# Merged first loads, an earlier warm-up, joined transposes, an ordered numerator and a split last accumulation in a two-layer decoder trunk

## The chip, the cores and the metric

The kernel runs on one core of one Trainium2 chip. The metric is device time in microseconds (us) for one launch of the whole program: the median of three runs.

## The reference

Two post-norm layers work on 256 tokens of width 1024 (float32). Each layer does a half-step SwiGLU feed-forward block, a token mixer beside a 4-head cross-attention into 256 memory tokens, and a second half-step feed-forward block. After each of the three sub-layers comes a LayerNorm:

```python
def swiglu(x, w_gate, w_up, w_down):
    return (silu(x @ w_gate) * (x @ w_up)) @ w_down        # 1024 -> 2816 -> 1024
for l in range(2):
    x = layer_norm(alpha * x + 0.5 * swiglu(x, ...), ...)
    u = x @ w_in                                            # one combined input projection
    tok = short_conv(u) if l == 0 else mlstm(u)             # 768 columns
    xa = cross_attention(u[..., -256:], mem @ w_kv[l])      # 256 columns
    x = layer_norm(alpha * x + concat(tok, xa) @ w_out, ...)
    x = layer_norm(alpha * x + 0.5 * swiglu(x, ...), ...)
```

In the mLSTM mixer of layer 1 each head's output is a numerator divided by the larger of the absolute denominator and a floor, and is then normalised over its 192 columns and multiplied by a sigmoid gate.

## The kernel before

**Precision.** Every float32 operand is split into a high part (ScalarE copies it to a rounded form, line 100) and a low part (VectorE subtracts the high part, line 101). A product is three matmuls: high by high, high by low, low by high (`mm3`, lines 176 to 178), or, in `mmw` (line 184), one 512-column and one 256-column matmul. So every weight tile that comes from memory passes through ScalarE and VectorE before TensorE may use it. The two casts of a 1 MB piece are each done in two halves of 1024 columns.

**Weights.** The list `pieces` holds all weight pieces in the order of their use, nearly all of 1 MB (128 partitions by 2048 columns). `get` traces the piece asked for and the one behind it: a load into one of three `raw` buffers by the SP queue, then the casts into one of five `wh` and five `wl` buffers. A `raw` buffer is free for the next load when its last low cast is done.

**The start.** VectorE clears a tile, ScalarE runs one Silu on one column of it, and 16 warm-up matmuls follow on TensorE (line 149). Then, for each of eight chunks of 128 input rows, SP issues one load of the tokens (128 KB, line 155) and one of the first feed-forward group's weights (256 KB, line 158), and both are cast. The first two groups (`outer`) run the chunk loop outermost, so that TensorE can start on the first chunk: four banks, and for each one 512- and one 256-column matmul. In even chunks the high part of the weight is used first, in odd chunks the low part. The second group's pieces (the third and the fourth of the list) are loaded in halves of 512 KB at line 133.

**The feed-forward blocks.** There are 11 groups of 256 hidden columns. In the three later blocks the first two groups (`xs_groups`) are computed token-major by `gu_xs`, for each half t of the tokens, and turned by two transposes each (`hx`, line 332, evacuated by ScalarE at 335 and VectorE at 336). The list `late` holds these transposes back by one step. Behind group 2 the remaining ones are done, and `down` multiplies groups 0 and 1 into the four output banks, token half 0 first. The last three groups' down products are done per token half and output half (`tail`), and `ln_half` and `ln_finish` follow.

**The mLSTM's end.** `numer(t, a)` computes two heads for a token half: matmuls (line 682), then a chain of small VectorE steps (lines 684 to 690), a power on GpSimd (line 691), and per head a VectorE multiply (line 694) and a ScalarE scaling (line 696). `tokens` transposes the result (line 718), ScalarE (262) and VectorE (263) evacuate it, and `OutProj.part` multiplies it by the four pieces of the output projection.

**What sets the order.** Each engine executes its instructions in one fixed order. That order is not the source's alone: a planner lays the program out by priority (source order) and modelled times, so a cast that is ready in its model can stand between two steps of an earlier chain. `tc.issue_after(ins)` makes the instructions that a block puts on the engine of `ins` stand behind `ins`, on that engine alone.

Of the kernel before, what the change touches and what calls it, by code (L numbers as in the profile page):

```python
# [8 lines left out]
F32 = mybir.dt.float32  # L9
F32R = mybir.dt.float32r  # L10
AF = mybir.ActivationFunctionType
# [3 lines left out]
P = 128  # L15
# [11 lines left out]
SPLIT = 1024  # L27
WARM = 16


@with_exitstack
def trunk(ctx: ExitStack, tc: tile.TileContext, d, out):
# [77 lines left out]
    def trace_piece(first=False):  # L110
        n = state["next"]
        if n >= len(pieces):
            return
        key, src, width = pieces[n]
        raw = rawp.tile([P, 2048], F32, tag="raw", name=f"raw{n}")
        state["next"] = n + 1
        if key == ("mem",):
            nc.sync.dma_start(raw, src)
            made[key] = new_act("memT")
            for q in range(2):  # L120
                split_act(raw[:, 1024 * q:1024 * q + 1024], made[key], 4 * q, 4)
            return
        h = wp.tile([P, 2048], F32R, tag="wh", name=f"wh{n}")
        l = wp.tile([P, 2048], F32R, tag="wl", name=f"wl{n}")
        made[key] = (h, l)
        if first:
            return raw, src, h, l
        if n >= 6:
            nc.sync.dma_start(raw[:, :width], src)
        for c in range(0, width, SPLIT):  # L130
            s = slice(c, min(c + SPLIT, width))
            if n < 6:
                nc.sync.dma_start(raw[:, s], src[:, s])
            split(raw[:, s], h[:, s], l[:, s])
# [10 lines left out]
    dve.memset(warm.bitcast(F32), 0.0)  # L145
    act.activation(warm[:, :1], warm[:, :1].bitcast(F32), AF.Silu)
    wb = mbank("warm")
    for _ in range(WARM):
        pe.matmul(wb[:, :256], warm[:, :P], warm, start=True, stop=True)
    x_raw = [zp.tile([P, D], F32, tag="z", name=f"xraw{q}") for q in range(2)]  # L150
    x0 = new_act("x0")
    first = [trace_piece(first=True) for _ in range(2)]
    for k in range(KC):
        xr = x_raw[k // 4][:, (k % 4) * T:(k % 4) * T + T]
        nc.sync.dma_start(xr, d["xT"][:, k * T:(k + 1) * T])
        raw, src, h, l = first[k // 4]
        s = slice((k % 4) * 512, (k % 4) * 512 + 512)
        nc.sync.dma_start(raw[:, s], src[:, s])
        split_act(xr, x0, k, 1)
        split(raw[:, s], h[:, s], l[:, s])  # L160
    cur = {"x": x0}
# [51 lines left out]
    def ln_half(i, t, h, y):  # L213
        if h == 0:
            lns[i, t] = (zp.tile([P, D], F32, tag="z", name=f"z{i}_{t}"),
                         sp.tile([P, 2, 6], F32, tag="st", name=f"st{i}_{t}"))
        z, st = lns[i, t]
        s = slice(512 * h, 512 * h + 512)
        dve.scalar_tensor_tensor(z[:, s], xnat[:, t, s], ALPHA, y, op0=ALU.mult, op1=ALU.add)
        dve.bn_stats(st[:, h, :], z[:, s])  # L220

    def ln_finish(i, t, gb, nx):
        z, st = lns.pop((i, t))
        mv = sp.tile([P, 2], F32, tag="mv", name=f"mv{i}_{t}")
        dve.bn_aggr(mv, st)
        r = rstd_of(mv[:, 1:2], 1, f"ln{i}_{t}")
# [9 lines left out]
        def transposes():  # L236
            for h in range(2):
# [4 lines left out]
                to_parts(nx, 4 * h, 4, t, b)  # L242
        return transposes

    def norm_both(i, gb, nx, tail):
# [20 lines left out]
    def ffn(l, j, xs_groups, i, last=False):  # L266
# [82 lines left out]
        for t in range(2):  # L349
            for g in range(xs_groups):  # L350
                late.append(gu_xs(g, t, pending if (t, g) == (0, xs_groups - 1) else None))
                if len(late) > 1:
                    late.pop(0)()
# [16 lines left out]
        def tail(t):  # L370
            for h in range(2):
                for g in range(NG - TAIL, NG):
                    down(g, t, (h,), ws[g])
                ln_half(i, t, h, y[t, h])
        norm_both(i, gb, nx, tail)


# [178 lines left out]
    def mlstm_mixer(mix, i):  # L556
# [113 lines left out]
        def numer(t, a):  # L670
# [18 lines left out]
            dve.scalar_tensor_tensor(v, r, EPS, r, op0=ALU.mult, op1=ALU.mult)  # L689
            dve.tensor_add(v, v, mv[:, :, 1])  # L690
            pool.tensor_tensor(r, v, mhalf[:, :2], op=ALU.pow)
            for c in range(2):
                o = ogs[t][:, DH * (2 * a + c):DH * (2 * a + c) + DH]
                dve.scalar_tensor_tensor(o, bv[:, c, :DH], mv[:, c, 0:1], o,
                                         op0=ALU.subtract, op1=ALU.mult)
                act.activation(o, o, AF.Copy, scale=r[:, c:c + 1])

# [53 lines left out]
        numer(0, 1)  # L751
        numer(1, 1)
        o.part(1, 1, (0, 1))
        for t in range(2):
            o.part(2, t, (0, 1), (0,))
        tokens(0, 1)
# [39 lines left out]
def _layouts(i):  # L796
# [5 lines left out]
    def colmajor(w, width):  # L802
# [3 lines left out]

    a["xT"] = c(i["x"][0].T.reshape(KC, P, T).transpose(1, 0, 2).reshape(P, KC * T))
    a["memT"] = c(i["mem"][0].T.reshape(KC, P, T).transpose(1, 0, 2).reshape(P, KC * T))
# [3 lines left out]
    g = g.reshape(2, 2, 2, 4, P, 2, NG, 256)  # L812
    a["wgu"] = c(g.transpose(0, 1, 6, 2, 4, 3, 5, 7).reshape(2, 2, NG, 2, P, 2048))
    a["wd"] = c(i["ffn_w_down"].reshape(2, 2, NG, 2, P, D).transpose(0, 1, 2, 4, 3, 5)
                .reshape(2, 2, NG, P, 2048))
# [32 lines left out]
```

## Time and profile before

| what | us |
|---|---|
| median of three runs (lowest, highest) | 987.87 (987.80, 988.37) |
| the profiled execution's own time | 988.58 |
| its span, first to last instruction | 986.4 |
| TensorE (PE) busy | 974.4 |
| VectorE (DVE) busy | 663.5 |
| ScalarE (ACT) busy | 528.9 |
| GpSimd (POOL) busy | 20.4 |

The profiled execution took 2.2 us more than its span, which lies around the first and last instruction, and 0.7 us more than the median. Matmuls are pipelined and their ends are modelled: what counts is the distance from one start to the next. "PEld" is the weight load, "SPq" an issue on the SP queue.

### The profile page before, as it was taken

To read this page: it belongs to the slowest core of one execution; us is meant where nothing else is said; L and a number is where in the kernel's file an instruction comes from. 1 tells how busy PE (TensorE), PEld (TensorE's weight loads), DVE (VectorE), ACT (ScalarE), POOL (GpSimd) and SP (SyncE) were. 2 spreads that over 40 slices of the span, in tenths; PEclk is the share of its full clock that TensorE was granted. 3 is DMA by queue.
4 is the path that set the end of the run, shared out by engine and by line. 5 is a ranking of instruction groups with operands and counts; after the bars stand their busy time and mean duration, and the time that the engine had idled before them with its cause. 6 is when DMAs were issued, how large, how long until landed. Compare 5 with 4: busy or idle time off the path is not lost.

```text
span 986.4 us, 13151 instructions
## 1 busy us (share of the span) xinstructions
PE 974.4 (99%) x5212; PEld 831.8 (84%) x5212; DVE 663.5 (67%) x1014; ACT 528.9 (54%) x847; POOL 20.4 (2%) x30
## 2 busy tenths in 40 slices
PE   8999999999999999999999999999999999999996
PEld 7888888888888888888888888889989778888885
DVE  6685657868667756565865656567878787566565
ACT  6665555447535545555455646445776446454540
POOL 0000000000000000000000000001000000000000
PEclk9999999999999999999999999999999999999999
DMA  8884646466444654646474555534425646546421
GB/s 284 315 302 167 217 168 218 170 225 219 165 155 173 248 202 149 228 153 214 145 282 171 183 201 176 198 113 149 162 95 198 247 175 242 202 154 221 164 86 44
DMA packets 29294, 186.92 MB, mean 189 GB/s; under 512 B 3632, under 2 KB 4656, under 8 KB 8368
## 3 DMA queue, kind: packets, MB, share of 16 engines
q1 hardware_dynamic: 28944, 185.55, 52.8%
q8 instruction: 41, 0.67, 0.3%
q10 hardware_dynamic: 288, 0.52, 0.1%
q14 instruction: 21, 0.17, 0.1%
HBM read 185.01 MB, written 1.05 MB: 189 GB/s over the span
## 4 chain that ended last, share of the span: by engine, by line
PE 97%; DMA 1%; DVE 1%; SPq 0%; ACT 0%; issue 0%; POOL 0%; DVEq 0%; POOLq 0%
PE gu L184 42%; PE y L176 8%; PE y L178 8%; PE y L177 8%; PE gx L176 2%; PE gx L178 2%; PE gx L177 2%; PE cx L184 2%; PE cg L184 2%; PE cb L184 2%; PE yo L178 1%; PE yo L177 1%; PE yo L176 1%; PE qkp L411 1%; PE qkp L412 1%; PE qkp L413 1%
## 5 line engine op out<-in xcount | busy, mean ns | idle before, releaser
L101 DVE TENSOR_TENSOR wl<-raw,wh 128x1024 fp32r<-128x1024 f32 (+1 forms) x342 | 400.1, 1196 | 147.0 <-ACT wh L100 146.4
L100 ACT ACTIVATE wh<-raw 128x1024 fp32r<-128x1024 f32 (+1 forms) x342 | 337.4, 1033 | 100.5 <-PE y L178 47.3
L184 PE MATMUL gu<-x,wh 128*128 128x512 f32 x1216 | 389.1, 395 | 0.0
L184 PEld LDWEIGHTS gu<-x,wl 128*128 128x128 f32 x1216 | 228.4, 188 | 52.9 <-DVE wl L101 1.8
L184 PE MATMUL gu<-x,wl 128*128 128x256 f32 x1216 | 243.3, 278 | 0.8 <-DVE wl L101 0.8
L184 PEld LDWEIGHTS gu<-x,wh 128*128 128x128 f32 x1216 | 189.6, 189 | 3.3
L176 PE MATMUL y<-wh,h 128*128 128x512 f32 x352 | 137.9, 392 | 0.0
L177 PE MATMUL y<-wl,h 128*128 128x512 f32 x352 | 137.0, 389 | 0.0
L178 PE MATMUL y<-wh,h 128*128 128x512 f32 x352 | 136.8, 390 | 0.0
L189 DVE TENSOR_TENSOR s<-s,gu 128x256 f32<-128x256 f32 x152 | 63.0, 417 | 101.7 <-ACT s L188 101.5
L188 ACT ACTIVATE s<-gu 128x256 f32<-128x256 f32 x152 | 57.5, 379 | 103.2 <-PE gu L184 103.2
L178 PEld LDWEIGHTS y<-wh,h 128*128 128x128 f32 x352 | 66.0, 188 | 14.3 <-DVE h L304 0.4
L177 PEld LDWEIGHTS y<-wl,h 128*128 128x128 f32 x352 | 66.1, 188 | 13.7
L176 PEld LDWEIGHTS y<-wh,h 128*128 128x128 f32 x352 | 66.1, 188 | 13.0 <-ACT h L303 0.7
L303 ACT ACTIVATE h<-s 128x256 fp32r<-128x256 f32 x76 | 31.7, 418 | 65.2 <-DVE s L300 64.9
L299 ACT ACTIVATE s<-s 128x256 f32<-128x256 f32 x76 | 31.7, 417 | 38.3 <-DVE s L189 38.3
L304 DVE TENSOR_TENSOR h<-s,h 128x256 fp32r<-128x256 f32 x76 | 32.0, 421 | 17.1 <-ACT h L303 16.9
L262 ACT ACTIVATE x<-xt 128x512 fp32r<-128x512 f32 x20 | 11.4, 596 | 51.4 <-PE xt L241 51.0
L176 PE MATMUL gx<-wh,x 128*128 128x512 f32 x96 | 38.3, 398 | 0.0
L177 PE MATMUL gx<-wl,x 128*128 128x512 f32 x96 | 37.5, 391 | 0.0
L178 PE MATMUL gx<-wh,x 128*128 128x512 f32 x96 | 37.5, 392 | 0.0
L300 DVE SCALAR_TENSOR_TENSOR s<-s 128x256 f32<-128x256 f32 x76 | 32.0, 421 | 1.4
(185 smaller groups left out, 977.5 us busy)
## 6 DMA issues: line engine op xcount, KB each, us to landing
raw<-in_wgu SPq DMA_DIRECT2D x83, 1024.0 KB, 4.8
raw<-in_wd SPq DMA_DIRECT2D x43, 1024.0 KB, 4.8
raw<-in_wconv SPq DMA_DIRECT2D x10, 1024.0 KB, 4.8
raw<-in_wout SPq DMA_DIRECT2D x8, 1024.0 KB, 4.8
raw<-in_wm SPq DMA_DIRECT2D x7, 1024.0 KB, 4.8
gb<-in_lngb SPq DMA_DIRECT2D x6, 1024.0 KB, 4.8
raw<-in_wkv SPq DMA_DIRECT2D x4, 1024.0 KB, 4.8
raw<-in_wop SPq DMA_DIRECT2D x4, 776.0 KB, 4.2
```

Source lines behind the costliest of these rows:

```text
L100: act.activation(h, raw, AF.Copy)
L101: dve.tensor_sub(l, raw, h.bitcast(F32))
L176: pe.matmul(o, ah, bh, start=start, stop=False)
L177: pe.matmul(o, ah, bl, start=False, stop=False)
L178: pe.matmul(o, al, bh, start=False, stop=stop)
L184: pe.matmul(o, w[part], b, start=(k, part) == (0, 0), stop=(k, part) == (KC - 1, 0))
L188: act.activation(o, bank[:, T:], AF.Copy)
L189: dve.tensor_add(o, o, bank[:, :T])
L299: act.activation(t_[:, :256], t_[:, :256], AF.Silu)
L300: dve.scalar_tensor_tensor(t_[:, 256:], t_[:, :256], 0.5, t_[:, 256:], op0=ALU.mult, op1=ALU.mult)
L303: act.activation(hh, t_[:, 256:], AF.Copy)
L304: dve.tensor_sub(hT[g][:, 1, fc, :], t_[:, 256:], hh.bitcast(F32))
```

## The change

The tokens and the first weights are laid side by side in one array (`xw`), so that one load per chunk brings both (384 KB). The first two chunks land in the two `z` buffers, the other six in the three `raw` buffers, two in each. The warm-up no longer waits for ScalarE, and has 20 matmuls; the Silu that loads ScalarE's table runs on a tile of its own, cleared by GpSimd. The transposes held in `late` are done two at a time. In `numer` the multiply and the scaling stand behind the chain of small steps, and the output projection's parts behind the last `numer` have their VectorE casts put behind that chain. In the last block, the last token half's second output half is accumulated in two steps for its last two groups: first columns 0 to 255, in the old bank, then columns 256 to 511, in a bank of their own, and `ln_close` adds the second in.

```diff
-WARM = 16
+WARM = 20
...
-    act.activation(warm[:, :1], warm[:, :1].bitcast(F32), AF.Silu)
     wb = mbank("warm")
     for _ in range(WARM):
         pe.matmul(wb[:, :256], warm[:, :P], warm, start=True, stop=True)
-    x_raw = [zp.tile([P, D], F32, tag="z", name=f"xraw{q}") for q in range(2)]
     x0 = new_act("x0")
     first = [trace_piece(first=True) for _ in range(2)]
+    CH = T + 512
+    xw = [zp.tile([P, D], F32, tag="z", name=f"xw{q}") for q in range(2)]
+    xw += [rawp.tile([P, 2048], F32, tag="raw", name=f"xw{q}") for q in range(2, 5)]
+    table = sp.tile([P, 1], F32, tag="table", name="table", bufs=1)
+    pool.memset(table, 0.0)
+    act.activation(table, table, AF.Silu)
     for k in range(KC):
-        xr = x_raw[k // 4][:, (k % 4) * T:(k % 4) * T + T]
-        nc.sync.dma_start(xr, d["xT"][:, k * T:(k + 1) * T])
-        raw, src, h, l = first[k // 4]
+        q, o = (k, 0) if k < 2 else (1 + k // 2, k % 2 * CH)
+        nc.sync.dma_start(xw[q][:, o:o + CH], d["xw"][:, k * CH:(k + 1) * CH])
+        h, l = first[k // 4]
         s = slice((k % 4) * 512, (k % 4) * 512 + 512)
-        nc.sync.dma_start(raw[:, s], src[:, s])
-        split_act(xr, x0, k, 1)
-        split(raw[:, s], h[:, s], l[:, s])
+        split_act(xw[q][:, o:o + T], x0, k, 1)
+        split(xw[q][:, o + T:o + CH], h[:, s], l[:, s])
...
+    def ln_close(i, t, y, y2):
+        z, st = lns[i, t]
+        dve.scalar_tensor_tensor(z[:, 512:], xnat[:, t, 512:], ALPHA, y, op0=ALU.mult, op1=ALU.add)
+        dve.bn_stats(st[:, 1, :], z[:, 512:768])
+        dve.tensor_add(z[:, 768:], z[:, 768:], y2)
+        dve.bn_stats(st[:, 2, :], z[:, 768:])
...
-                if len(late) > 1:
+                if len(late) > 2:
+                    late.pop(0)()
                     late.pop(0)()
...
+            down(NG - TAIL, t, (1,), ws[NG - TAIL])
+            y2 = mbank("ylast")[:, :256]
+            ends = [(g, fc) for g in range(NG - TAIL + 1, NG) for fc in range(2)]
+            for q, o in enumerate((y[1, 1][:, :256], y2)):
+                for n, (g, fc) in enumerate(ends):
+                    s = slice(fc * D + 512 + 256 * q, fc * D + 768 + 256 * q)
+                    mm3(o, (hT[g][:, 0, fc, tsl(t)], hT[g][:, 1, fc, tsl(t)]),
+                        (ws[g][0][:, s], ws[g][1][:, s]), (q, n) == (1, 0), n == len(ends) - 1)
+            ln_close(i, t, y[1, 1], y2)
...
-            dve.tensor_add(v, v, mv[:, :, 1])
+            chain = dve.tensor_add(v, v, mv[:, :, 1])
             pool.tensor_tensor(r, v, mhalf[:, :2], op=ALU.pow)
-            for c in range(2):
...
+            with tc.issue_after(chain.ins):
+                for c in range(2):
...
+            return chain.ins
...
-        numer(1, 1)
-        o.part(1, 1, (0, 1))
-        for t in range(2):
-            o.part(2, t, (0, 1), (0,))
+        with tc.issue_after(numer(1, 1)):
+            o.part(1, 1, (0, 1))
+            for t in range(2):
+                o.part(2, t, (0, 1), (0,))
```

## Rows read from the trace of the kernel before

**Rows 1.** The page: busy time, share and instructions of each engine, and the shares of the chain that ended last.

```profile
PE 974.4 (99%) x5212; PEld 831.8 (84%) x5212; DVE 663.5 (67%) x1014; ACT 528.9 (54%) x847; POOL 20.4 (2%) x30
...
PE 97%; DMA 1%; DVE 1%; SPq 0%; ACT 0%; issue 0%; POOL 0%; DVEq 0%; POOLq 0%
```

**Rows 2.** The chain that ended last, in order of time, two pieces of its start: start, duration, what.

```profile
9.33 7.19 DMA raw<-in_wgu
...
18.92 11.05 PE gu L184 x62
```

**Rows 3.** The timeline of TensorE at the start: start, duration, engine, line, operation, out<-in, shape, count (rows of one kind are merged), and in brackets the idle time and what ended it.

```profile
2.27 3.74 PE L149 MATMUL warm<-warm 128*128 128x256 f32 x16 [2.27 <-ACT warm L146]
5.85 0.41 PE L184 MATMUL gu<-x,wh 128*128 128x512 f32 x1
...
7.15 0.28 PE L184 MATMUL gu<-x,wl 128*128 128x256 f32 x1
8.19 0.38 PE L184 MATMUL gu<-x,wl 128*128 128x256 f32 x1 [0.76 <-DVE wl L101]
...
17.98 0.86 PE L184 MATMUL gu<-x,wh 128*128 128x512 f32 x3
18.92 0.51 PE L184 MATMUL gu<-x,wl 128*128 128x256 f32 x2
```

**Rows 4.** The timeline of ScalarE and VectorE in the same stretch: the clearing of the warm-up tile, and the casts of the first chunks.

```profile
0.85 0.27 DVE L145 MEMSET warm<- 128x256 f32 x1 [0.85 <-PEq L840]
...
4.40 0.63 ACT L100 ACTIVATE wh<-raw 128x512 fp32r<-128x512 f32 x1 [0.76 <-DMA raw<-in_wgu]
...
5.07 0.69 DVE L101 TENSOR_TENSOR wl<-raw,wh 128x512 fp32r<-128x512 f32 x1 [0.97 <-ACT wh L100]
...
5.55 0.42 ACT L100 ACTIVATE x<-xraw 128x256 fp32r<-128x256 f32 x1 [0.52 <-DMA xraw<-in_xT]
...
6.78 0.63 ACT L100 ACTIVATE wh<-raw 128x512 fp32r<-128x512 f32 x1 [0.81 <-DMA raw<-in_wgu]
...
7.44 0.69 DVE L101 TENSOR_TENSOR wl<-raw,wh 128x512 fp32r<-128x512 f32 x1 [1.02 <-ACT wh L100]
```

**Rows 5.** The timeline of the SP queue: the issues of the first chunk's tokens and of the second chunk's weights (those of the first chunk's weights and of the second's tokens lie between).

```profile
0.73 0.39 SPq L155 DMA_DIRECT2D xraw<-in_xT  x1
...
2.10 0.43 SPq L158 DMA_DIRECT2D raw<-in_wgu  x1
```

**Rows 6.** Two stretches of the table by windows: stretch and length, busy time and instructions of each engine, granted clock, share of the DMA engines, GB/s. The rows loaded in the first are 1 and 2 KB long, in the second 4 KB.

```profile
2.00:4.00 2.00, 1.73 (x8) 1.73 (x9) 0.33 (x1) 0.62 (x3) 0.00 (x0) 1.00 0.89 230
...
16.00:18.00 2.00, 2.00 (x14) 1.65 (x13) 1.02 (x2) 1.45 (x3) 0.00 (x0) 1.00 1.06 404
```

**Rows 7.** The timeline of TensorE behind the last numerators.

```profile
782.46 0.39 PE L178 MATMUL yo<-wh,mix 128*128 128x512 f32 x1
782.69 0.49 PE L718 MATMUL tk<-ident,og 128*128 128x128 f32 x3
783.76 0.50 PE L176 MATMUL yo<-wh,mix 128*128 128x512 f32 x1 [0.58 <-ACT mix L262]
...
785.64 0.39 PE L178 MATMUL yo<-wh,mix 128*128 128x512 f32 x1
```

**Rows 8.** The timelines of VectorE, GpSimd and ScalarE there: the last step of the last numerator's chain and the cast ahead of it, two of the four powers, and the scaling that the transposes wait for.

```profile
781.26 1.23 DVE L101 TENSOR_TENSOR wl<-raw,wh 128x1024 fp32r<-128x1024 f32 x1 [0.65 <-ACT wh L100]
782.40 0.15 DVE L690 TENSOR_TENSOR dv<-dv,hmv 128x2 f32<-128x2 f32 x1
...
778.48 0.69 POOL L691 TENSOR_TENSOR dn<-dv,mhalf 128x2 f32<-128x2 f32 x1 [18.20 <-DVE dv L690]
782.73 1.51 POOL L691 TENSOR_TENSOR dn<-dv,mhalf 128x2 f32<-128x2 f32 x1 [3.56 <-DVE dv L690]
...
784.28 0.80 ACT L696 ACTIVATE og<-og,dn 128x192 f32<-128x192 f32 x2 [0.57 <-POOL dn L691]
```

**Rows 9.** The timeline of TensorE around one pair of transposes (the matmul before, and the second matmul behind), and one piece of the chain with eight transposes.

```profile
503.42 0.39 PE L178 MATMUL gx<-wh,x 128*128 128x512 f32 x1
...
504.10 0.39 PE L177 MATMUL gx<-wl,x 128*128 128x512 f32 x1
...
310.53 0.87 PE xt L241 x8
```

**Rows 10.** The second feed-forward block, behind group 2: VectorE's low part of the last transposes, and the fifteenth matmul of `down` on TensorE.

```profile
337.95 0.42 DVE L336 TENSOR_TENSOR h<-hx,h 128x256 fp32r<-128x256 f32 x1
...
338.82 0.39 PE L178 MATMUL y<-wh,h 128*128 128x512 f32 x1
```

**Rows 11.** The end of the kernel: two VectorE steps of the timeline, two groups of VectorE instructions by shape (busy time, mean ns of one, idle time before), and two pieces of the chain, a matmul of 256 columns and one of 512, each up to the next one's start.

```profile
978.65 0.69 DVE L219 SCALAR_TENSOR_TENSOR z<-xnat,y 128x512 f32<-128x512 f32 x1 [2.34 <-PE y L178]
979.37 0.69 DVE L220 BATCH_NORM_STATS2 st<-z 128x6 f32<-128x512 f32 x1
...
L189 DVE TENSOR_TENSOR s<-s,gu 128x256 f32<-128x256 f32 x152 | 63.0, 417 | 101.7 <-ACT s L188 101.5
L684 DVE BATCH_NORM_STATS2 hst<-num 128x6 f32<-128x192 f32 x8 | 2.6, 353 | 1.1 <-PE num L682 1.1
...
759.96 0.12 PE qkp L413
...
970.00 0.23 PE y L177
```

More of the change, by code (lines that the diff above doesn't have):

```diff
@@ L114, in trace_piece @@
         key, src, width = pieces[n]
-        raw = rawp.tile([P, 2048], F32, tag="raw", name=f"raw{n}")
         state["next"] = n + 1
+        if not first:
+            raw = rawp.tile([P, 2048], F32, tag="raw", name=f"raw{n}")
         if key == ("mem",):
@@ L126, in trace_piece @@
         if first:
-            return raw, src, h, l
+            return h, l
         if n >= 6:
@@ L215, in ln_half @@
             lns[i, t] = (zp.tile([P, D], F32, tag="z", name=f"z{i}_{t}"),
-                         sp.tile([P, 2, 6], F32, tag="st", name=f"st{i}_{t}"))
+                         sp.tile([P, 3, 6], F32, tag="st", name=f"st{i}_{t}"))
         z, st = lns[i, t]
@@ L224, in ln_finish @@
         mv = sp.tile([P, 2], F32, tag="mv", name=f"mv{i}_{t}")
-        dve.bn_aggr(mv, st)
+        dve.bn_aggr(mv, st if nx is None and t == 1 else st[:, :2, :])
         r = rstd_of(mv[:, 1:2], 1, f"ln{i}_{t}")
@@ L371, in tail @@
             for h in range(2):
+                if last and (t, h) == (1, 1):
+                    break
                 for g in range(NG - TAIL, NG):
@@ L374, in tail @@
                 ln_half(i, t, h, y[t, h])
+            else:
+                return
+            down(NG - TAIL, t, (1,), ws[NG - TAIL])
[7 more added lines that the diff above has]
+            ln_close(i, t, y[1, 1], y2)
         norm_both(i, gb, nx, tail)
@@ L689, in numer @@
             dve.scalar_tensor_tensor(v, r, EPS, r, op0=ALU.mult, op1=ALU.mult)
-            dve.tensor_add(v, v, mv[:, :, 1])
+            chain = dve.tensor_add(v, v, mv[:, :, 1])
             pool.tensor_tensor(r, v, mhalf[:, :2], op=ALU.pow)
-            for c in range(2):
[L693 to L696, printed above, removed]
+            with tc.issue_after(chain.ins):
+                for c in range(2):
+                    o = ogs[t][:, DH * (2 * a + c):DH * (2 * a + c) + DH]
+                    dve.scalar_tensor_tensor(o, bv[:, c, :DH], mv[:, c, 0:1], o,
+                                             op0=ALU.subtract, op1=ALU.mult)
+                    act.activation(o, o, AF.Copy, scale=r[:, c:c + 1])
+            return chain.ins
         v1 = [hp.tile([P, NH, DH + 1], F32, tag="h", name=f"v1_{t}") for t in range(2)]
@@ L805, in colmajor @@
         return c(w.reshape(KC, P, n, width).transpose(2, 1, 0, 3).reshape(n, P, KC * width))
-    a["xT"] = c(i["x"][0].T.reshape(KC, P, T).transpose(1, 0, 2).reshape(P, KC * T))
     a["memT"] = c(i["mem"][0].T.reshape(KC, P, T).transpose(1, 0, 2).reshape(P, KC * T))
@@ L813, in _layouts @@
     a["wgu"] = c(g.transpose(0, 1, 6, 2, 4, 3, 5, 7).reshape(2, 2, NG, 2, P, 2048))
+    xT = i["x"][0].T.reshape(KC, P, T).transpose(1, 0, 2)
+    w0 = a["wgu"][0, 0, 0].reshape(2, P, 4, 512).transpose(1, 0, 2, 3).reshape(P, KC, 512)
+    a["xw"] = c(np.concatenate([xT, w0], axis=2).reshape(P, KC * (T + 512)))
     a["wd"] = c(i["ffn_w_down"].reshape(2, 2, NG, 2, P, D).transpose(0, 1, 2, 4, 3, 5)
```

## The prediction

> **What bounds the kernel now.** I read the page first: TensorE is busy for 974.4 of 986.4 us, and the chain that ended last runs for 97% through it [rows 1]. So nothing that spares ScalarE, VectorE or a transfer in the middle is worth anything by itself; time can come only from the 12 us in which TensorE doesn't work, and from TensorE instructions that go. Then I read the chain in order of time, and TensorE's timeline where it isn't on that chain. There are three such places. At the start the chain passes through the load of the third weight piece (7.19 us from its issue) before TensorE takes it over at 18.92 for good [rows 2]. Behind the last numerators TensorE waits twice within 3 us [rows 7]. At the end VectorE works alone, normalising the last half [rows 11]. All terms are made against the profiled execution, 988.58 us (a span of 986.4 and 2.2 around it), which lies 0.71 above the median of 987.87; I carry the sum over to the median. No change of this kernel below 0.2% (1.98 us) is told from none here.
>
> **The start.** Now: 16 warm-up matmuls begin at 2.27, behind ScalarE, and the first real one at 5.85 [rows 3]: (5.85 - 2.27) / 16 = 0.22 each for 256 columns, where 256 columns later take 0.12 [rows 11]. [...] The last matmul of chunk 0 starts at 7.15 and takes 0.12, and the next starts at 8.19: 0.92 lost, since chunk 1 begins with the low part of its weights, whose cast runs from 7.44 to 8.13 [rows 3, 4]. Just before 18.92, three matmuls of 0.23 from 17.98 end at 18.67: 0.25 lost to the third piece's casts; between the two places I count 0.1 more in uneven spacings, an estimate. [...] ScalarE's Silu on its own tile costs nothing: ScalarE has no other work until the first load lands. The first load's issue stays at 0.73, and the second chunk's weights, issued at 2.10 now [rows 5], go with the second load, one issue of about 0.45 behind the first: near 1.2. The chunk's weights now land at about 4.38 and 6.76, which is where ScalarE stops waiting for them [rows 4]. A load of 384 KB lands as a whole, so the tokens' cast (0.42) no longer runs ahead of the weights: that is the change's own cost. A chunk's low part is ready at its landing plus 0.42 + 0.63 + 0.69 and three hand-overs, 1.9 together. The rows loaded grow from 1 and 2 KB to 3 KB; the 1 and 2 KB rows went at 230 GB/s with the DMA engines 0.89 busy, 4 KB rows at 404 [rows 6]; I take 330 for 3 KB, nearer the middle than either end. Then the first chunk lands near 4.1 and the second, 393 KB and 1.2 us behind it plus what several loads in flight cost each other, near 5.7. Chunk 0 starts near 5.3, and chunk 1's low part is ready at 7.6 in place of 8.13. From there TensorE has 1.4 us of work per chunk against about 1.2 of load and 1.1 of casts on either engine, so it doesn't wait again. Gain: 0.55 at chunk 1, the 0.35 behind it, and 0.1 because the third piece no longer shares the queue with the last chunks: 1.0. Ends: 0, if the second chunk lands as now; at most the 1.27 lost plus 0.5 of earlier start, 1.8. A loss is possible too, since the third piece's buffer is free only when chunk 3 is cast: it would be requested near 10 instead of 9.33 [rows 2], 0.7 later, all of which could reach TensorE.
>
> [...]
>
> **Joined transposes.** A pair costs TensorE this: from 503.42 to 504.10 there are 0.68 us and two matmuls of 0.23, which leaves 0.22, or 0.11 for one transpose; eight in a row take 0.87, again 0.11 each [rows 9]. So a visit has no cost of its own that joining could save: 0. Ends: a gain of 0.02 for each of two visits saved in three blocks, 0.1; a loss if the evacuation comes late. Group 0's transposes for token half 1 now come behind group 2 with those of group 1. They are needed from the thirteenth matmul of `down` on, their low part in the fifteenth, which starts at 338.82; VectorE finishes the low part there at 338.37 [rows 10]. The cover is 0.45 us in the order of now.
>
> **Numerators.** From 782.69 to 785.64 TensorE does six transposes (6 x 0.11) and five matmuls (5 x 0.23): 1.8 of 2.95 us, so 1.15 are lost [rows 7]. The first wait, 0.58, is for ScalarE's evacuation of the first transposes. The second is for the last numerator's scaling at 784.28, behind a power of 1.51, behind a chain step at 782.40 that stood behind a cast of 1.23 [rows 8]. With the chain ahead of the multiplies and of the output projection's casts I expect that step near 780, two to three us earlier; the power takes 0.70 and the scaling 0.80 [rows 8], so the second token half is ready by 783, when TensorE has done the first three transposes. All six then follow one another, the evacuation's wait stays, and the sixth matmul starts at 783.76 + 5 x 0.23 = 784.9 instead of 785.64. I take 0.65. Ends: a gain of 1.15 if the planner moves the transposes ahead of other work; a loss, because the edge holds back the casts of the output projection's last piece (two of 1.23) until the chain is done, with everything behind them in VectorE's queue. If the step stays at 782.40, they end near 784.9, and the first triple's third matmul, which needs VectorE's evacuation behind them, comes about 1.2 late. The casts of the next block aren't in that block and may still cut in.
>
> **The end.** Twelve matmuls of 512 columns become 24 of 256: 24 x 0.12 - 12 x 0.23 = +0.12. Behind the last one VectorE now adds 512 columns (0.69) and takes their statistics (0.69) [rows 11]. After, that work on the finished columns lies beside the second 12 matmuls (1.44), and an add of 256 columns (0.42) and statistics of 256 remain; 192 columns take 0.35, so 0.40 [rows 11]. 1.41 - 0.03 - 0.82 is a gain of 0.56, less 0.12 and about 0.04 for a wider aggregate: 0.4. Ends 0.2 and 0.6: only VectorE's first two steps running over the 1.44 could shorten it, and they take 1.1.
>
> **The sum.** -1.0 - 0 - 0.65 - 0.4 = -2.05: 986.5 for the profiled execution, and 985.8 against the median.
>
> **The rivals.** *The start is held by its transfers:* the DMA engines are 0.9 busy from 2 us on [rows 6], one load must bring tokens and weights before anything is cast, and the third piece is asked for later. The gain there is 0, the rest 1.05: 986.8. Against it stands that 404 GB/s is reached with longer rows. *The numerators gain nothing:* the held casts or the next block's stand beside the power. The power took 0.69 once and 1.51 when a cast of two SBUF operands ran beside it [rows 8]; forcing casts directly behind the chain invites just that, and the 0.65 is used up. The sum is -1.4: 986.5. [...] *More than that, at the start and the numerators:* the second chunk lands at 5.4 (0.3 more), and the planner, with an earlier chain in its model, lifts the transposes so that the 0.58 goes too: -2.95, 984.9. *Slower:* the joined transposes' low part comes too late. At three blocks VectorE would have to finish two evacuations where one had 0.45 us to spare; one more pair of casts (2 x 1.23) ahead of them costs 2.46 + 0.42 - 0.45 = 2.4 each, one cast 1.2. With one cast in each block, +3.6 - 2.05 = +1.55: 989.4, with two in one of them 990.6. It decides from 0.45 us of delay on. Against it: the evacuation stands ahead of the next cast in all likelihood, since it comes earlier in the source.
>
> **How the numbers follow.** The forecast has 0.48, and its own range of 985.0 to 986.7 lies across the bound at 985.89, two thirds below it: 0.32 faster, 0.16 same. The better case has 0.15, faster. The held start (0.15) and the idle numerators (0.14) are within 0.2%. The slower case has 0.08, 0.05 of it above 989.85. That gives 0.47 faster, 0.48 same, 0.05 slower. The range leaves out most of the slower case and the outer ends of the start: 984.3 to 988.0.
>
> **What would show it.** The start: TensorE's first real matmul near 5.3, chunk 1 near 7.6, and the work that is at 18.92 now near 17.9. The transposes: four in 0.44 and no wait in `down`. The numerators: the chain's last step near 780, and no wait for the scaling. The end: from the last matmul's start to the aggregate 1.3 in place of 1.9. It is wrong if chunk 1 starts at 8.1 or later, if new waits for VectorE appear on TensorE behind group 2, or if the planner's order has changed far from the edits.

## The result, and the profile after

The changed kernel is slower: 990.47 us (median of 11 executions, 989.55 to 993.69) against 988.20 for the kernel before (11 executions, 987.73 to 989.06), a ratio of 1.0025 with a 95% interval of 1.0017 to 1.0033. That is 2.3 us the wrong way, 4.7 above the forecast of 985.8 and 2.5 above the upper end of its range, 988.0. The profiled execution of the changed kernel took 992.05 (span 989.8). TensorE's granted clock fell once in it, and its mean over the span is 0.994, as in the slowest execution (993.69); the nine others have 0.997 or 0.998. How far the fall counts is told with the experiments.

Read in the order of time, three of the four places went about as forecast. The start, from TensorE's timeline and from the chain that ended last (start, duration, what; idle time and its releaser in brackets):

```profile
5.47 0.63 PE L189 MATMUL gu<-x,wh 128*128 128x512 f32 x2
...
7.33 0.40 PE L189 MATMUL gu<-x,wh 128*128 128x512 f32 x1
...
9.88 0.80 PE L189 MATMUL gu<-x,wl 128*128 128x256 f32 x2
```

```profile
2.10 6.45 DMA xw<-in_xw
...
10.29 18.54 PE gu L189 x104
...
34.30 10.81 PE gu L189 x62
```

The first real matmul is at 5.47 (5.85 before) and chunk 1 has begun by 7.33 (8.19) [rows 3]. A fourth load now lands at 8.55 and holds TensorE a last time near 9.9. From 10.29 it runs without a stop, past the place near 18.9 where the chain of before was still waiting [rows 2]. The group that starts at 34.30 started at 35.43 before: 1.13 gained. But that is one profile against one. e2 and e8 (below) keep the start of before, and their profiles reach the same group earlier than that of the kernel before; here are before, e2 and e8, from the same chain:

```profile
35.43 11.18 PE gu L184 x64
```

```profile
34.53 11.18 PE gu L184 x64
```

```profile
34.80 11.18 PE gu L184 x64
```

The ten profiles with the new start lie between 33.93 and 34.77. So the profile that the forecast was made from was the latest of three, and by these thirteen profiles the usual gain is nearer to half a microsecond.

The joined transposes, one group of them in the chain of the second feed-forward block:

```profile
334.21 0.44 PE hx L345 x4
```

Four transposes take 0.44, 0.11 each as in [rows 9], and no matmul behind them waits.

The numerators, from the timelines of TensorE, VectorE and GpSimd:

```profile
782.01 0.82 PE L747 MATMUL tk<-ident,og 128*128 128x128 f32 x6
783.08 0.50 PE L181 MATMUL yo<-wh,mix 128*128 128x512 f32 x1 [0.25 <-ACT mix L275]
```

```profile
777.23 0.69 POOL L718 TENSOR_TENSOR dn<-dv,mhalf 128x2 f32<-128x2 f32 x1 [16.69 <-DVE dv L717]
779.16 0.69 POOL L718 TENSOR_TENSOR dn<-dv,mhalf 128x2 f32<-128x2 f32 x1 [1.24 <-DVE dv L717]
```

The chain's last step came at 778.83 instead of 782.40 [rows 8], both powers took 0.69, all six transposes follow one another, and 0.25 of marked waiting is left where the kernel before has 0.58 [rows 7] and 0.29:

```profile
784.78 0.33 PE L718 MATMUL tk<-ident,og 128*128 128x128 f32 x1 [0.29 <-ACT og L696]
...
792.70 0.39 PE L178 MATMUL yo<-wh,mix 128*128 128x512 f32 x1
793.02 1.29 PE L241 MATMUL xt<-ident,xnat 128*128 128x128 f32 x8
```

The lead over the kernel before grows from 0.68 at the transposes (782.69 - 782.01) to 1.52 at the last `yo` matmul (792.70 - 791.18): 0.84 gained.

Then all of it is lost, and more, within 10 us. TensorE behind that point:

```profile
791.18 0.39 PE L183 MATMUL yo<-wh,mix 128*128 128x512 f32 x1
794.49 1.94 PE L246 MATMUL xt<-ident,xnat 128*128 128x128 f32 x8 [2.92 <-DVE xnat L236]
797.29 0.63 PE L181 MATMUL gx<-wh,x 128*128 128x512 f32 x1
...
800.89 0.39 PE L181 MATMUL gx<-wh,x 128*128 128x512 f32 x1
```

The transposes of the normalised tokens (`xt`) wait 2.92 us for VectorE's `xnat`; the kernel before has no such wait, as its row at 793.02 above shows. The table by windows (length, busy time of PE, PEld, DVE, ACT, POOL, granted clock, DMA share, GB/s) shows what came behind the wait:

```profile
794.00:796.00 2.00, 1.51 (x7) 1.54 (x8) 2.00 (x4) 0.38 (x1) 0.00 (x0) 0.50 0.00 0
...
800.00:802.00 2.00, 2.00 (x9) 1.63 (x8) 2.00 (x4) 0.00 (x0) 0.28 (x1) 0.85 0.78 262
```

The two stretches between them show 0.50 as well. From 797.29 to 800.27 the `gx` matmuls start 0.43 apart, from 800.89 on, with a granted clock of 1.00 from 802 to 804, 0.23. The second set of eight transposes starts at 807.9; before it was 804.1.

VectorE in the same stretch, with the ten microseconds ahead of it:

```profile
770.34 0.56 DVE L693 SCALAR_TENSOR_TENSOR decays<-ms,decays 128x384 f32<-128x384 f32 x1 [4.94 <-PE ms L692]
772.02 0.56 DVE L693 SCALAR_TENSOR_TENSOR decays<-ms,decays 128x384 f32<-128x384 f32 x1 [1.12 <-PE ms L692]
775.41 0.63 DVE L711 BATCH_NORM_STATS2 hst<-num 128x6 f32<-128x192 f32 x2 [2.83 <-PE num L709]
...
779.56 3.49 DVE L101 TENSOR_TENSOR wl<-raw,wh 128x1024 fp32r<-128x1024 f32 x3
...
784.00 2.35 DVE L101 TENSOR_TENSOR wl<-raw,wh 128x1024 fp32r<-128x1024 f32 x2
...
786.86 1.22 DVE L101 TENSOR_TENSOR wl<-raw,wh 128x1024 fp32r<-128x1024 f32 x1
...
789.57 0.69 DVE L224 SCALAR_TENSOR_TENSOR z<-xnat,yo 128x512 f32<-128x512 f32 x1 [0.30 <-PE yo L183]
...
791.61 0.69 DVE L224 SCALAR_TENSOR_TENSOR z<-xnat,yo 128x512 f32<-128x512 f32 x1
792.22 0.15 DVE L211 TENSOR_SCALAR ln_0v<-mv 128x1 f32<-128x1 f32 x1
...
793.60 1.41 DVE L236 SCALAR_TENSOR_TENSOR xnat<-z,ln_0r,gb 128x512 f32<-128x512 f32 x2
```

VectorE stands idle for 8.9 us (4.94 + 1.12 + 2.83) ahead of the numerators, and then runs six casts of weights between 779.56 and 788.0, the last one between two steps of token half 0's LayerNorm. At 791.61 a step of token half 1 stands ahead of half 0's `ln_0v`, which needed nothing by then but its place in the queue. That step reads what the last `yo` matmul has written, so it could not start before TensorE had run out of work. In the chain it stands, and no cast, between that matmul and half 0's path:

```profile
791.35 0.24 PE yo L183
...
791.61 0.69 DVE z L224
```

From 791.61 to `xt` at 794.49 there are 2.9 us, the whole wait of this profile. So half 1's step sets the end of the wait here; the cast at 786.86 and the step of half 1 at 789.57, which itself waits for TensorE, delay half 0's statistics ahead of it. The held casts hold their buffers too, and so the loads behind them. ScalarE, which makes the high part first, waits for data there:

```profile
791.77 2.00 ACT L100 ACTIVATE wh<-raw 128x1024 fp32r<-128x1024 f32 x2 [3.03 <-DMA raw<-in_wgu]
```

The end, VectorE behind the last matmul, which starts at 982.28:

```profile
982.60 0.42 DVE L255 TENSOR_TENSOR z<-z,ylast 128x256 f32<-128x256 f32 x1 [0.29 <-PE ylast L183]
...
983.52 0.24 DVE L230 BATCH_NORM_AGGREGATE mv<-st 128x2 f32<-128x18 f32 x1
```

From the last matmul's start to the aggregate there are 1.24 us, in place of 1.88 (980.10 - 978.22) before, whose steps of 512 columns are in [rows 11]. From the first of the last half's matmuls to the end of the span it is 15.71 instead of 16.11: 0.40 gained.

So the trace gives -1.13, 0, -0.84 and -0.40 where -1.0, 0, -0.65 and -0.4 were forecast, and a wait of 2.92 with a fall of the clock behind it that was not in the sum. The places add up: 1.52 ahead of the kernel before at the last `yo` matmul, 1.47 behind at `xt`, 3.8 behind at the second set, and 3.4 behind at the end of the span. (Of the start's 1.13 only 0.68 were left at the numerators. Most of the rest goes near 680, where the chain of this profile passes through a load of weights, 5.30 us from 670.95, and that of before does not.) My theory: the edges shift VectorE's queue, so that casts stand ahead of half 0's LayerNorm, on which TensorE then waits. The rivals: the loss is a ripple of the start or the transposes; the numerators' own order makes it; or half 1's steps make it and the casts don't matter.

### The profile page after: what moved, and what is told of

Read it like the earlier page. It is cut to its first block, busy times and chain, and to the rows that moved or that the text cites. A ratio compares the mean times of both kernels' runs of the same rounds, so it can differ in the third digit from the quotient of the medians.

```text
span 989.8 us, 13168 instructions
## 1 busy us (share of the span) xinstructions
PE 977.7 (99%) x5228; PEld 836.0 (84%) x5228; DVE 664.2 (67%) x1016; ACT 528.5 (53%) x847; POOL 19.6 (2%) x31
## 4 chain that ended last, share of the span: by engine, by line
PE 96%; DMA 2%; DVE 1%; ACT 0%; issue 0%; SPq 0%; DVEq 0%; ACTq 0%
PE gu L189 42%; PE y L181 8%; PE y L183 8%; PE y L182 8%; PE gx L181 2%; PE gx L182 2%; PE gx L183 2%; PE cx L189 2%; PE cg L189 2%; PE cb L189 2%; PE yo L181 1%; PE qkp L438 1%; PE yo L182 1%; PE yo L183 1%; PE qkp L439 1%; PE qkp L440 1%
## 5 line engine op out<-in xcount | busy, mean ns | idle before, releaser
L101 DVE TENSOR_TENSOR wl<-raw,wh 128x1024 fp32r<-128x1024 f32 x334 | 394.4, 1207 | 141.8 <-ACT wh L100 141.1
L100 ACT ACTIVATE wh<-raw 128x1024 fp32r<-128x1024 f32 x334 | 332.3, 1042 | 95.0 <-PE y L183 28.5
L181 PE MATMUL y<-wh,h 128*128 128x512 f32 (+1 forms) x352 | 137.5, 391 | 0.0
L182 PE MATMUL y<-wl,h 128*128 128x512 f32 (+1 forms) x352 | 136.6, 388 | 0.0
L183 PE MATMUL y<-wh,h 128*128 128x512 f32 (+1 forms) x352 | 136.5, 389 | 0.0
```

Source lines behind the costliest of these rows:

```text
L100: act.activation(h, raw, AF.Copy)
L101: dve.tensor_sub(l, raw, h.bitcast(F32))
L181: pe.matmul(o, ah, bh, start=start, stop=False)
L182: pe.matmul(o, ah, bl, start=False, stop=False)
L183: pe.matmul(o, al, bh, start=False, stop=stop)
```

## The experiments

All ratios are against the kernel before on the same chip. In e1, e3, e4, e5, e6, e9, e10 and e11 the changed kernel is the base, in e2, e7 and e8 the kernel before.

**e1: without both edges.**

```diff
-            with tc.issue_after(chain.ins):
-                for c in range(2):
+            for c in range(2):
...
-        with tc.issue_after(numer(1, 1)):
-            o.part(1, 1, (0, 1))
+        numer(1, 1)
+        o.part(1, 1, (0, 1))
```

> The changed kernel without its two edges on VectorE (the multiplies of og may stand between the chain's steps again, and the casts of the output projection's last piece are no longer kept behind the chain); start, joined transposes and end stay. Theory (the held casts push the casts of the next weights into the LayerNorm of token half 0): TensorE's idle time of 2.92 us before the transposes xt near 794 goes, the granted clock behind it stays near 1.00, and the time is that of the kernel before less what start and end give, 988.2 - 1.1 - 0.4 = 986.7, 986.0 to 987.4. Rival 1 (the loss is a ripple of the start or of the joined transposes, and the edges only happen to stand there): the idle time and the low clock stay, near 990.5. Rival 2 (start and end give nothing in timed runs): 988.2.

Measured: 987.03 (986.87 to 987.39), ratio 0.9985, interval 0.9976 to 0.9993. The casts are back in VectorE's free time (the first pair and the last of five are shown, two single ones lie between), and `xt` follows the last `yo` matmul (791.42) without a wait:

```profile
764.73 2.35 DVE L101 TENSOR_TENSOR wl<-raw,wh 128x1024 fp32r<-128x1024 f32 x2
...
773.15 1.23 DVE L101 TENSOR_TENSOR wl<-raw,wh 128x1024 fp32r<-128x1024 f32 x1 [1.16 <-ACT wh L100]
```

```profile
791.75 1.29 PE L246 MATMUL xt<-ident,xnat 128*128 128x128 f32 x8
```

The five casts (2.35 + 3 x 1.22, 6.0 us of work) stand where the changed kernel has 8.9 us of nothing. Both rivals of this run fall: the loss sits in the edges, and the other three parts together are a gain.

**e2: the kernel before, with nothing but the casts held.**

```diff
-        numer(1, 1)
+        with tc.issue_after(numer(1, 1)):
+            o.ws[2] = get("wo", 1, 2)
         o.part(1, 1, (0, 1))
```

> The kernel before with one thing added: the low casts of the output projection's last piece stand behind the chain of numerator (1,1) on VectorE; the numerators are as before, and so are start, transposes and end. Theory (held casts alone make the loss): an idle time of 1.5 to 3 us before xt, a granted clock near 0.5 behind it, and 1.5 to 4 us more than before: 989.7 to 992.2. Rival (the order inside the numerators makes it): 988.2, no idle time before xt over 0.3 us.

Measured: 990.52 (989.82 to 991.73), ratio 1.0020, interval 1.0011 to 1.0029. The numerators' own steps keep their order of before, and the wait is there; behind it, in the profiled execution, the `gx` matmuls start 0.43 apart from 795.86 to 798.84, as they do in the changed kernel at a granted clock of 0.50:

```profile
782.88 0.50 PE L176 MATMUL yo<-wh,mix 128*128 128x512 f32 x1 [0.25 <-ACT mix L262]
...
793.88 1.29 PE L241 MATMUL xt<-ident,xnat 128*128 128x128 f32 x8 [2.51 <-DVE xnat L231]
```

So holding the casts is enough to make the loss. It is enough for the numerators' gain too: no cast stands between the chain's steps any more, the six transposes follow one another, and the wait behind them is the 0.25 of the changed kernel.

**e10 and e11: one edge each.** These two complete the square. e10 takes away the outer edge only, e11 the inner one only.

> The changed kernel without the outer edge alone (the casts of the output projection's last piece are free), the inner one (multiplies of og behind the chain) stays. VectorE's order then has four casts of weights between the chain's steps of the last two numerators, and one cast and one z and bn_stats of half 1 among the steps of half 0's LayerNorm. Theory (each cast in a chain costs its 1.2 us where the chain is waited for): the transposes tk of token half 1 wait again as in the kernel before, xt waits 0.5 to 2 us, and the time lies between e1 and the changed kernel, 987.3 to 989.5. Rival (the inner edge gives its gain without the outer one): 986.0 to 986.8.

> The changed kernel without the inner edge alone (the multiplies of og may stand between the chain's steps), the outer one stays: with e1 (neither edge), e10 (inner only) and the changed kernel (both) this fills the square. VectorE's order has two held casts, one more, and two z of half 1 (one of them between the steps of half 0) and a cast ahead of half 0's normalisation, as in e2. Theory: the wait before xt is that of e2 (2.5 us, clock falling in a part of the executions), and the time is e2's 990.5 less what start and end give, 1.3: 989.2, 988.5 to 990.2. Rival (only the inner edge does harm): 987.0.

Measured: e10 992.40 (990.59 to 993.30, 5 executions), ratio 1.0037, interval 1.0024 to 1.0051; e11 990.61 (988.87 to 991.08), ratio 1.0019, interval 1.0010 to 1.0028. Both lie above what the theory expected, e10 by 2.9 us and e11 by 0.4, and both rivals fall. `xt` waits 2.51 us in e11, as in e2. In e10 the output projection's casts ran early, but VectorE's order has other casts inside the last numerators' chains and one ahead of half 0's normalisation, where it waited for its high part:

```profile
792.84 1.23 DVE L101 TENSOR_TENSOR wl<-raw,wh 128x1024 fp32r<-128x1024 f32 x1 [0.36 <-ACT wh L100]
793.99 1.41 DVE L234 SCALAR_TENSOR_TENSOR z<-z,mv,gb 128x512 f32<-128x512 f32 x2
```

```profile
796.20 1.29 PE L246 MATMUL xt<-ident,xnat 128*128 128x128 f32 x8 [3.13 <-DVE xnat L236]
```

The held casts are therefore a sufficient cause and not the only one: either edge alone changes the planner's order of VectorE's queue, and each of these orders puts something ahead of half 0's path. What the theory has to say is "whatever stands in the queue ahead of half 0", not "the held casts". The square also parts the gain: the numerators' waits are 0.25 with the outer edge alone (e11), and 0.58 and 0.53 with the inner edge alone (e10), no less than before. The gain comes with the casts being held back, and so does the wait that ate it.

**e6: half 1's LayerNorm steps kept behind half 0's.** The edit names only the order of these steps.

```diff
+        with tc.issue_after(done[0]) if i == 4 and t == 1 else ExitStack():
+            dve.scalar_tensor_tensor(z[:, s], xnat[:, t, s], ALPHA, y, op0=ALU.mult, op1=ALU.add)
+            dve.bn_stats(st[:, h, :], z[:, s])
...
+            done[0] = dve.scalar_tensor_tensor(xnat[:, t, s], z[:, s], r, gb[:, 1, s],
+                                               op0=ALU.mult, op1=ALU.add).ins
```

> The changed kernel with the same edge alone (half 1's z and bn_stats behind half 0's last xnat); the casts of the output projection's last piece stay held back, and VectorE's order has four casts of weights between the last numerator and the first z and three more among half 0's steps, against two in the changed kernel. Theory (the pile of held casts makes the wait, and the order of half 1's steps adds to it): three casts of 1.2 us among the steps keep the wait over 1.5 us, the clock falls again, 989.5 to 991. Rival (half 1's steps alone make the wait): the wait goes, 986.2 to 987.4.

Measured: 990.12 (989.67 to 991.44), ratio 1.0020, interval 1.0011 to 1.0029. The casts took the place of half 1's steps (three stand among half 0's steps, where the changed kernel has one), and the wait is as long as ever:

```profile
794.28 1.29 PE L248 MATMUL xt<-ident,xnat 128*128 128x128 f32 x8 [3.00 <-DVE xnat L238]
```

So moving half 1's steps, which set the wait in the changed kernel's profile, is not enough: the wait doesn't hang on them alone. The clock, which was expected to fall again, did not fall in this profiled execution:

```profile
794.00:796.00 2.00, 1.66 (x10) 1.14 (x10) 2.00 (x5) 1.05 (x2) 0.00 (x0) 1.00 0.93 360
```

**e4: TensorE kept busy through the wait.** 24 matmuls on zeros stand between the last `yo` matmul and `xt`.

```diff
+                    for _ in range(FILL):
+                        f = pe.matmul(fb[:, :256], warm[:, :P], warm, start=True, stop=True)
+                with tc.issue_after(f.ins):
+                    tr()
```

> The changed kernel, with 24 matmuls of 256 columns on zeros put on TensorE between the last matmul of the output projection and the transposes xt, where it stood idle for 2.92 us; VectorE's order is that of the changed kernel. Theory (the second half of the loss is the granted clock of 0.50 behind the idle time, and the idle time brings it): the clock stays near 1.0, gx matmuls take 0.23 us instead of 0.43, xt starts at most 0.4 us later, and the time is 990.5 - 2.9 + 0 to 0.4 = 987.6 to 988.0. Rival (the clock falls there for another reason): the gx matmuls stay at 0.43 and the time is 990.5 to 990.9.

Measured: 989.79 (989.15 to 990.28), ratio 1.0014, interval 1.0005 to 1.0023; a miss of 1.8 us. The clock stayed at 1.00 and the matmuls at 0.23, with `xt` where it was:

```profile
791.44 3.03 PE L270 MATMUL fill<-warm 128*128 128x256 f32 x24
794.53 1.29 PE L249 MATMUL xt<-ident,xnat 128*128 128x128 f32 x8
```

```profile
796.00:798.00 2.00, 1.87 (x7) 1.01 (x8) 2.00 (x4) 2.00 (x3) 0.00 (x0) 1.00 0.00 0
```

Against the changed kernel's profile the second set of transposes comes 1.7 earlier (806.2 for 807.9). None of its executions lies above 990.28, where seven of the changed kernel's eleven do. Both speak for a fall that the idle stretch brings, at 1.7 us in the executions that have it, and against the rival. They don't prove it: e6's profile shows no fall either, without any filling. The miss is in the price: the expectation took 2.9 us off for the clock, and TensorE's wait for `xnat` is still there, filled with work that nothing needs.

**e3, e5, e9: the casts let free, and then one queue after the other put in order.** e3 keeps both edges but traces the output projection's last two pieces ahead of numerator (1,1), and holds the next feed-forward piece's casts behind the chain instead. e5 adds e6's edge. e9 adds one on ScalarE: two high casts of a later piece behind half 0's copies of x.

```diff
+        o.ws[2] = get("wo", 1, 2)
+        o.ws[3] = get("wo", 1, 3)
+        held[0] = numer(1, 1)
+        with tc.issue_after(held[0]):
...
+                with tc.issue_after(held[0]) if (l, j, g) == (1, 1, 0) else ExitStack():
+                    xsw[g] = [get("gu", l, j, g, 0)]
+                with tc.issue_after(xcopy[0]) if (l, j, g) == (1, 1, 1) else \
+                        tc.issue_after(held[0]) if (l, j, g) == (1, 1, 0) else ExitStack():
+                    xsw[g].append(get("gu", l, j, g, 1))
```

> The changed kernel with its edges on the numerators' steps, but the last two pieces of the output projection are traced ahead of numerator (1,1), so that the casts of its last piece and of the first feed-forward piece run in VectorE's free time ahead of the numerators; the next feed-forward pieces' low casts are kept behind the chain. Theory: the wait for xnat and the low clock go, the numerators keep their 0.8 us, and the time is 986.7 - 0.8 = 985.9, 985.3 to 986.6. Rival (the numerators' order itself brings LayerNorm late): idle time before xt stays over 1.5 us and the time is 989 or more.

> The kernel of e3 with one edge more: in the LayerNorm behind the output projection, the steps z and bn_stats of token half 1 stand behind the last xnat of token half 0 on VectorE. In e3 one z and one bn_stats of half 1 (0.69 and 0.70 us, with 0.19 of waiting for TensorE) stood between ln_0v and the normalisation, and TensorE waited 1.54 us for xnat. Theory (the order in VectorE's queue, not the amount of work, sets that wait): the wait falls to 0.3 us or less, and the time is 988.5 - 1.3 to 1.6 = 986.9 to 987.2, and down to 986.2 if the numerators' 0.85 comes through whole against e1 (987.0). Rival (the wait moves to the low half of x, which the same engine makes, or to half 1's LayerNorm): 988.0 to 988.6.

> The kernel of e5 with one edge on ScalarE: the two high casts of the fourth-next feed-forward piece stand behind the two copies of x for token half 0. In e5 xt no longer waited for xnat, but the four high casts of weights (789.79, 3.90 us) stood ahead of the copies of x on ScalarE, which were over only at 794.66, and TensorE waited 1.81 us for them; the granted clock fell to 0.50 behind that wait in the profiled execution. Theory (the wait goes from queue to queue until every step of half 0's path stands ahead of the weights' casts): with the copies at 791.8 instead of 793.6 the wait falls to 0.3 us or less, the clock stays near 1.00, and the time is that of e1 less up to 0.85 that the numerators give: 986.1 to 987.0. Rival (a fourth queue takes it, the low half of x on VectorE or the loads): 987.8 to 989.

e3 measured 988.47 (988.12 to 989.50), ratio 1.0004, interval 0.9995 to 1.0013: 2 us better than the changed kernel and 2 worse than expected. No cast is left among half 0's steps, and a z and a bn_stats of half 1 took the place, between `ln_0v` at 788.60 and the normalisation at 790.28:

```profile
788.95 0.69 DVE L225 SCALAR_TENSOR_TENSOR z<-xnat,yo 128x512 f32<-128x512 f32 x1 [0.19 <-PE yo L183]
789.67 0.70 DVE L226 BATCH_NORM_STATS2 st<-z 128x6 f32<-128x512 f32 x1
```

```profile
792.49 1.29 PE L247 MATMUL xt<-ident,xnat 128*128 128x128 f32 x8 [1.54 <-DVE xnat L237]
```

e5 measured 989.85 (987.89 to 990.62), ratio 1.0011, interval 1.0001 to 1.0020, above the theory's range and above the rival's. The wait for `xnat` went as expected, but a queue that neither had named took it, ScalarE's:

```profile
789.79 3.90 ACT L100 ACTIVATE wh<-raw 128x1024 fp32r<-128x1024 f32 x4 [6.84 <-PE yo L183]
793.60 1.06 ACT L278 ACTIVATE x<-xt 128x512 fp32r<-128x512 f32 x2
```

```profile
791.12 1.29 PE L249 MATMUL xt<-ident,xnat 128*128 128x128 f32 x8
794.22 0.50 PE L181 MATMUL gx<-wh,x 128*128 128x512 f32 x1 [1.81 <-ACT x L278]
```

The transposes are done by 792.4, and their copies stand behind four high casts of weights. In this profiled execution the clock fell (the `gx` matmuls start 0.43 apart from 795.07 to 798.05), and cost some 1.5 us beside the wait of 1.81: from the first `gx` matmul to the second set of transposes there are 11.26 us (794.22 to 805.48), against 9.81 before (794.34 to 804.15).

e9 measured 986.04 (985.74 to 986.74), ratio 0.9974, interval 0.9965 to 0.9983, within what the theory expected. The copies of x stand behind two high casts instead of four, TensorE shows no wait between `xt` (791.76) and `gx`, and the clock is 1.00 from 786 to 804:

```profile
790.50 2.01 ACT L100 ACTIVATE wh<-raw 128x1024 fp32r<-128x1024 f32 x2 [6.84 <-PE yo L183]
792.42 1.26 ACT L279 ACTIVATE x<-xt 128x512 fp32r<-128x512 f32 x2
```

It is the fastest version measured, about 2.6 us (0.0026 x 988) better than the kernel before, and it holds the change whole, with three positions in the queues put right besides.

**e7 and e8: start alone, end alone.**

> The kernel before with the new start alone (20 warm-up matmuls, table load behind the first issues, one load per chunk). By the traces TensorE's work of the first stage should end 1.1 us earlier, and nothing behind it takes that back: 988.26 - 1.1 = 987.2, 986.6 to 987.7. Rival (the later weight loads are what sets the pace, so the gain is lost at the next wait): 988.0 to 988.4.

> The kernel before with the new end alone (last 256 columns in a bank of their own). From the last matmul to the end of the span the trace should show 0.4 us less than before, with the pair of adds and statistics of 256 columns in place of one z and one bn_stats of 512; one time cannot resolve that, 987.5 to 988.3. Rival (the smaller steps cost as much as they save): the stretch behind the last matmul is as long as before.

e7 measured 987.80 (987.07 to 990.61), ratio 0.9997, interval 0.9988 to 1.0006. Its first real matmul starts at 5.39 and its profiled span is 984.9, against 986.4 in the profile of before, but by the ratio only 0.3 is gained, and the median lies just above the theory's range (to 987.7). The interval (-1.2 to +0.6) holds the forecast of -1.0 and also no gain at all. The traces suggest why it is less than 1.1: e7's group starts at 33.93, which is 1.5 ahead of the profile of before, and 0.6 and 0.9 ahead of those of e2 and e8. e8 (one time, 987.65) confirms its step in the trace: 15.77 from the last half's first matmul to the end of the span, 0.34 less than before.

## Why the prediction was wrong

**The start (-1.0): right against the one profile that it was made from, in part by luck.** 1.13 at the group behind it, first matmul and chunk 1 close to the forecast; "it doesn't wait again" from chunk 1 on was wrong by one more wait near 9.9. The term lived on losses of 0.92 and 0.25 in that profile. In e2 and e8, with the same start, chunk 0's first matmuls of 512 columns are 0.43 from the next start instead of 0.24, and no wait is marked at chunk 1; against these two the changed kernel gains 0.2 and 0.5. e1, with start, transposes and end, is 1.5 faster (interval 0.7 to 2.4) where 1.4 were forecast, and e7's interval for the start alone reaches from a gain of 1.2 to a loss of 0.6. So the rival of the held start did not come in the traces, and the times don't exclude it.

**Joined transposes (0): right.** 0.11 each as before, no wait. The slower rival was laid there: a low part late behind casts in VectorE's queue. A step of that kind, late behind other work in VectorE's queue, is what made the kernel slower, but at another place, the LayerNorm behind the output projection.

**The end (-0.4): right**, 0.40 in the changed kernel, 0.34 in e8.

**Numerators (-0.65): the step that failed.** Its inner working held: the chain was earlier, the powers took 0.69, and 0.84 was gained at the output projection. The forecast was lower because it counted one matmul too many: from 782.69 to 785.64 four start (783.76, 784.10, 784.87 and 785.32), not five, so 1.37 us were lost there and not 1.15. It had also laid the gain on both edges, and e10 and e11 give it to the outer one. The rival of the idle numerators fell with it: the power that started at 779.16, ahead of the first cast at 779.56, took 0.69, where the one of before, which started at 782.73 beside a cast that ran from 782.48 to 783.70, took 1.51. Nor did the casts take longer beside it: three take 3.49 there, and 3.49 at 805.27 too, where GpSimd does nothing. Why the power of before took 1.51 no run here shows.

What failed is the bound on the loss. I saw that the edge holds back the casts "with everything behind them in VectorE's queue", and priced it at about 1.2 on one condition, that the chain's step stays at 782.40; I ended the list of those who wait at the next evacuation. The chain's step came at 778.83, so the condition was not met, and the loss came all the same. I didn't ask what these casts did in the 8.9 us ahead of the numerators in which VectorE has nothing else, nor who waits for the queue 10 us later: half 0's LayerNorm, behind which everything stands that TensorE has left in its order. The term was +2.9 of waiting, and some 2 more where the clock fell, in place of a bound of 1.2.

The prediction named as a sign of error "if the planner's order has changed far from the edits". It had: e10 and e11 show that each edge alone brings an order that costs 2.5 to 3.1 of waiting at the same place, and e9 that with three queue positions mended a gain of the forecast's size is there, 2.6 us (interval 1.7 to 3.5) against 2.05. That is another kernel than the one forecast; it shows that the terms of the sum were to be had, not that the forecast was right.

## What to carry to other kernels

An edge that holds a block behind one instruction holds all that the block traces on that engine, loads' casts included: list them, find in the timeline which idle time they filled, and follow the pile that they make to the next step that the bounding engine cannot do without. When a planner orders the queues, compare its whole order behind an edit, not only at the edit; the wait, 2.92 us in the changed kernel, passed here from queue to queue as it was mended (from VectorE's casts to half 1's steps, 1.54 in e3, and to ScalarE's casts, 1.81 in e5) until the path of the first half stood far enough ahead of the work that is not urgent (none in e9). A gain of under a microsecond is worth its edge only if what the edge pushes back has that much slack behind it. And read a term of under a microsecond from more than one profile of the kernel before: the same start differed by 0.9 us between three of them.

## What the runs showed of the hardware

The granted clock fell from 1.00 to 0.50 behind idle stretches of TensorE of 2.92 (the changed kernel), 2.51 (e11) and 3.13 us (e10). Behind 2.51 in e2, and in e5 behind 1.81 us of idle time with eight transposes ahead of it, the `gx` matmuls were 0.43 apart, as at 0.50 in the changed kernel, in place of 0.23. In the changed kernel the clock stayed low, 0.50 in the windows from 794 to 800 and 0.85 in the next one, although TensorE was busy again from 794.49. It did not fall behind 3.00 us in e6's profiled execution (1.00 from 794 to 798), nor, by matmuls that stay 0.23 apart, behind 1.54 in e3's. So the length of the idle stretch alone doesn't decide it; what does, no run here shows. The executions of one kernel differ too: e5's times lie in two groups, 987.89 to 988.47 (4 executions) and 989.79 to 990.62 (7), e11's at 988.87 to 989.12 (3) and 990.37 to 991.08 (8); their means are 1.9 and 1.7 apart. In e11 the mean granted clock is 0.999 in the three and 0.996 or 0.997 in the eight.

At the start of the kernel the granted clock of the table says less than the matmuls do: it reads 1.00 from 2 to 4 us [rows 6], where the warm-up matmuls of 256 columns start 0.22 apart, against 0.12 later. That the warm-up ran as at a granted 0.50 is my estimate from the spacing alone: 0.22 / 0.12 is 1.8, and 0.43 / 0.23, behind the wait in the changed kernel, is 1.9.
